# Fourth up product's operands first, bank reads first in a stage's first block, and a residual load in two halves: a fp32 decoder trunk on one core

## The chip, the core and the metric

One NeuronCore of a Trainium2 chip runs the whole program. The metric is device time in microseconds, the median of several executions; lower is better. TensorE does matrix products, VectorE (DVE) and ScalarE (ACT) do elementwise work, GpSimd (POOL) does small work and issues accumulating transfers, SyncE (SP) issues plain transfers.

## What is computed

Two decoder layers over 512 tokens of width 1024, in fp32. Layer 0 mixes with latent attention, layer 1 with banded attention; each layer ends in a squared-ReLU MLP, with a layer norm behind the mixer and one behind the MLP.

```
for l in range(2):
    y = mla(x, ...) if l == 0 else swa(x, shared_kv, ...)
    x = layernorm(alpha * x + y, ln_mix_g[l], ln_mix_b[l])
    h = relu(x @ mlp_w_up[l])            # 1024 -> 4096
    x = layernorm(alpha * x + (h * h) @ mlp_w_down[l], ln_mlp_g[l], ln_mlp_b[l])
```

## The kernel before, in words

Each fp32 operand is split into a high and a low part (`split`, L74: ACT writes the high part, DVE subtracts to give the low one), and each product is three matmuls: high by high, high by low, low by high. So a tile of weights (128x1024, 512 KB) costs a load, one ACT and one DVE instruction before TensorE can use it. The tiles pass in one `stream` through a ring of four pairs `wh`, `wl`; `weights(name)` (L295) hands out the next tile and prepares up to four ahead, but none beyond `state["hold"]`.

The order of the work on each engine is made by a scheduler ahead of the run, from priorities in program order and its own estimate of times. `tc.high_priority()` lifts instructions ahead of others that are ready; `pe(...)` and `pin(...)` keep an instruction behind what was traced before it on its engine; `behind(pair)` (L84) queues a block behind the two instructions of a split. On the chip every engine but TensorE's weight loads takes its instructions strictly in that order.

A projection back to tokens (`TokMajor`, L425) does the first 512 output columns in parts, and then in `finish` (L451) the last 512: for each block of 128 tokens 24 matmuls over four weight tiles, the addition into `xs[t]`, and the layer norm. `xs` and the norm's gain and bias `gb` come over SP. `finish` may pin the norm's DVE work (`early`).

The MLP runs in four blocks of 1024 hidden columns, each as seven products instead of eight (Strassen's scheme). An up product `U` is 48 matmuls of 256 columns, a down product `D` 24 matmuls of 512. A dash marks the block that is being begun; `FIRST_STEPS` (L40) begins with U'1 U'2 U'5 U'3 U'6 U'7 U'4 D'1 D'2, so U'3 is the fourth up product. `XFactors.turn` (L609) transposes a token block and forms the factors of U'1, U'2 and U'5; at the last one it forms those of U'3, 6, 7 and 4. Weight tiles of the sums are grown in place: POOL adds the next quarter to the raw tile by an accumulating DMA (L188) once the last split has read it. `up_out` (L694) reads the banks: for U'6 the sums L709, L710, L712, for U'7 L715, for U'4 L718. U'4 adds onto the bank of U'7, so it can't begin a half before L715 has read that half. D'1 needs the first hidden quarter (L712, then ReLU and square on ACT, L720 and L721, then the split of its factor in L730).

`begin` (L548) starts the second layer's mixer: three weight chunks by two halves of the tokens; `src.turn` puts the transposed token blocks 2 and 3 in place, which the second half reads.

Of the kernel before, what the change touches and what calls it, by code (L numbers as in the profile page):

```python
# [15 lines left out]
P = 128  # L16
# [32 lines left out]
def build(tc, nc, io, out):  # L49
    with ExitStack() as top:  # L50
# [40 lines left out]
        def pe(ins):  # L91
            tc.keep_in_program_order(ins)
# [71 lines left out]
        def queue_seven(name, key, chunk):  # L164

            quads = {}

            def half(a, jp):  # L170
                if a not in quads:
                    if (key, a) == ("U", "a"):
                        quads[a] = xp.tile([P, 4, 512], F32, tag="xt", bufs=8, name=nm("wq"))
                    elif (key, a) == ("U", "b"):
                        quads[a] = xtok.tile([P, 4, 512], F32, tag="gb", bufs=1, name=nm("wq"))
                    else:
                        quads[a] = mlp_pool[0].tile([P, 4, 512], F32, tag="quad" + a, bufs=1, name=nm("wq"))
                return quads[a][:, 2 * jp : 2 * jp + 2, :]

            def flat(ap):  # L180
                return ap.rearrange("p a b -> p (a b)")

            def grown(a, jp, *more, aside=None):
                wh, wl = tiles_of_weights(aside)
                with behind(state.pop("first", None) if (key, a, jp) == ("U", "b", 1) else None):
                    split(wh, wl, flat(half(a, jp)), keep=(a, bool(more)) == ("b", True) and key == "U")
                if more:
                    nc.gpsimd.dma_start(half(a, jp), chunk(*more, jp), accum_op=ALU.add)  # L188
                return wh, wl

            def loaded(a, jp, at, *more, aside=None):
                pe(nc.sync.dma_start(half(a, jp), chunk(*at, jp)))
                return grown(a, jp, *more, aside=aside)

            def alone(jp, aside=None):
                raw = raw_tile()
                pe(nc.sync.dma_start(raw.rearrange("p (a b) -> p a b", a=2), chunk(1, 0, jp)))
                wh, wl = tiles_of_weights(aside)
                split(wh, wl, raw)
                return wh, wl  # L200

            of = {
                1: lambda jp, aside=None: loaded("a", jp, (0, 0), 0, 1, aside=aside),
                5: lambda jp: grown("a", jp, 1, 1),
                6: lambda jp: grown("a", jp, 1, 0),
                4: lambda jp: grown("a", jp),
                2: alone,
                3: lambda jp: loaded("b", jp, (1, 1), 0, 1),
                7: lambda jp: grown("b", jp),
            }  # L210

            def add(n, asides=(None, None)):
                for jp, aside in enumerate(asides):
                    make = (lambda jp=jp, aside=aside: of[n](jp, aside)) if aside else (lambda jp=jp: of[n](jp))
                    stream.append((name, make))
                    off_ring.append(aside is not None)

            return add
# [48 lines left out]
        mlp_stream(0)  # L267
        for m in range(2):
            queue("w_k", io["w_k"][m])
        first_sq = len(stream)  # L270
        for m in range(8):
            queue("w_sq", io["w_sq"][m], nc.gpsimd if m else nc.vector)
            if m == 0:
# [151 lines left out]
        class TokMajor:  # L425
# [25 lines left out]
            def finish(self, gb=None, dst=None, early=None):  # L451

                for kp in range(4):
                    for t in range(NT):
                        if (t, kp) not in self.done:
                            self.part(t, kp)
                if gb is not None:
                    gb = gb()  # L460
                    ws = [weights(self.name) for _ in range(4)]
                    for t in range(NT):
                        n = 2 if dst is None and t == NT - 1 else 1
                        for i in range(n):
                            c = slice(i * 512 // n, (i + 1) * 512 // n)
                            b = bank(512 // n)
                            for kp in range(4):
                                self.group(b, t, kp, ws[kp], c)
                            pinned[0] = early
                            with tc.high_priority():  # L470
                                self.evac(t, slice(512 + c.start, 512 + c.stop), b)
                            pinned[0] = False
                        pinned[0] = early
                        with tc.high_priority():
                            layer_norm(t, gb, dst)
                        if early:
                            prepare(early[t])
                        pinned[0] = False
                        if dst is not None and t in (1, 2):
                            with tc.high_priority():  # L480
                                dst.turn(t - 1)
                else:
                    bs = [bank() for _ in range(NT)]
                    for kp in range(4):
                        w = weights(self.name)
                        for t in range(NT):
                            self.group(bs[t], t, kp, w)
                    for t in range(NT):
                        self.evac(t, slice(512, D), bs[t])
# [58 lines left out]
        def begin(src, chunks):  # L548


            state["hold"] = len(stream)
            ws = [weights(name) for name, _ in chunks]
            for half_ in range(2):
                cols = slice(half_ * 256, half_ * 256 + 256)
                for i, (_, evac) in enumerate(chunks):
                    b = bank(256)
                    early = half_ == 0 and i == len(chunks) - 1
                    feat_major(src, ws[i], b, cols, range(4))
                    if early:
                        with tc.high_priority():  # L560
                            src.turn(NT - 1)
                    feat_major(src, ws[i], b, cols, range(4, KD))
                    evac(cols, b)
                    if half_ == 0 and i == 1:
                        with tc.high_priority():
                            src.turn(NT - 2)


        class Factors:
# [24 lines left out]
        class XFactors(Factors):  # L594
# [14 lines left out]
            def turn(self, t):  # L609
# [18 lines left out]
                if t == NT - 1:  # L628
                    state["hold"] = len(stream)
                    quarters = [f32(self.xf[i][:, n]) for i in range(2) for n in range(2)]  # L630
                    first = split(self.part(3, 0), self.part(3, 1), self.sum(3, *quarters))
                    with behind(first):
                        for n in (6, 7, 4):
                            split(self.part(n, 0), self.part(n, 1), self.sum(n, *quarters))
                    state["first"] = first

        def mlp(src, gb, dst, mp):

# [16 lines left out]
            class Block:  # L655
# [18 lines left out]
                def up(self, n):  # L674
                    w = [weights("up") for _ in range(2)]
                    key = {3: 3}.get(n) or own_bank[n]
                    for j in range(4):

                        b = self.bank(("U", key), j // 2)
                        wh, wl = w[j // 2]  # L680
                        for k in range(4):
                            c = slice(j % 2 * 512 + k * P, j % 2 * 512 + (k + 1) * P)
                            group(
                                b[:, j % 2 * 256 : j % 2 * 256 + 256],
                                three(wh[:, c], wl[:, c], src.part(n, 0)[:, k, :], src.part(n, 1)[:, k, :]),
                                n not in (2, 4) and k == 0 and j % 2 == 0, k == 3, skip_group_check=True,
                            )
                        if j % 2:
                            self.up_out(n, j // 2)
                        if (self.q, j) == (0, 1) and n in (1, 2):  # L690
                            with tc.high_priority():
                                src.turn(n + 1)
# [80 lines left out]
            for i, (which, q, n) in enumerate(steps):  # L773
                if which == "U":
                    blocks[q].up(n)
                else:
                    blocks[q].down_(n)
                    if (q, n) == (NFF - 2, 6):
# [21 lines left out]
                    n = ((2, 1), (4, 0))[cols.start // 256][k // 4]  # L800
                    return b.fac[n][:, p, k % 4, cols.start % 256 : cols.start % 256 + P]

            if dst is not None:
                state["hold"] = first_sq
            TokMajor(Hidden(), add_last, "down").finish(gb, dst, dst and (0, 0, 0, 1))


        ed = dr.tile([SQH, BANDW], F32, name="ed")
# [290 lines left out]

        for t in range(NT):  # L1100
            xs[t] = xtok.tile([P, D], F32, tag="x", bufs=NT, name=nm("x"))
            pe(nc.sync.dma_start(xs[t], io["x"][t * P : (t + 1) * P, :]))
        gb = lambda: load_gb(io["ln_mix_g"][0], io["ln_mix_b"][0])
        x2 = Feat()
        with tc.tile_pool(name="mlp0", bufs=1) as mp:
            mlp_pool[0] = mp
# [288 lines left out]
```

## Time and profile before

| | us |
|---|---|
| median of 3 runs | 1025.76 (1025.19 to 1031.15) |
| profiled execution | 1023.86 |
| its span, first to last instruction | 1021.9 |
| TensorE busy | 994.6 (97%) |
| DVE busy | 766.6 (75%) |
| ACT busy | 555.9 (54%) |

The span is what the profile covers; 2.0 us of the profiled execution lie around it. Busy times of TensorE count overlapping matmuls once, so idle shows as a gap between the starts of two matmuls that is longer than their usual spacing.

### The profile page before, as it was taken

To read this page: it belongs to the slowest core of one execution; us is meant where nothing else is said; L and a number is where in the kernel's file an instruction comes from. 1 tells how busy PE (TensorE), PEld (TensorE's weight loads), DVE (VectorE), ACT (ScalarE), POOL (GpSimd) and SP (SyncE) were. 2 spreads that over 40 slices of the span, in tenths; PEclk is the share of its full clock that TensorE was granted. 3 is DMA by queue.
4 is the path that set the end of the run, shared out by engine and by line. 5 is a ranking of instruction groups with operands and counts; after the bars stand their busy time and mean duration, and the time that the engine had idled before them with its cause. 6 is when DMAs were issued, how large, how long until landed. Compare 5 with 4: busy or idle time off the path is not lost. (4 is left out here: it accounts for less than half of the span.)

```text
span 1021.9 us, 15865 instructions
## 1 busy us (share of the span) xinstructions
PE 994.6 (97%) x6148; PEld 895.9 (88%) x6148; DVE 766.6 (75%) x1227; ACT 555.9 (54%) x847; POOL 232.9 (23%) x204
## 2 busy tenths in 40 slices
PE   9999999989999999999999999999899999999996
PEld 8888887987999989998889898889799999998986
DVE  6588856888769858886585578688886896797756
ACT  5556643456637637646146688445654664665620
POOL 1232001312211211210014675223032122123002
PEclk9999999999999999999999999999999999999998
DMA  7421108389877976972332212349688798798332
GB/s 247 149 85 42 63 21 268 87 191 243 154 172 199 190 178 180 243 125 94 113 103 94 83 64 73 119 87 227 175 182 168 164 227 160 183 258 153 84 124 82
DMA packets 60247, 149.55 MB, mean 146 GB/s; under 512 B 5212, under 2 KB 9741, under 8 KB 60173
## 3 DMA queue, kind: packets, MB, share of 16 engines
q0 software_dynamic: 24320, 58.73, 32.1%
q1 hardware_dynamic: 35852, 89.82, 25.6%
q8 instruction: 48, 0.79, 0.3%
q14 instruction: 27, 0.21, 0.1%
HBM read 146.41 MB, written 4.22 MB: 147 GB/s over the span
## 5 line engine op out<-in xcount | busy, mean ns | idle before, releaser
L103 PE MATMUL mm<-wh,fac 128*128 128x512 f32 (+1 forms) x944 | 295.5, 390 | 4.6 <-ACT fac L76 3.0
L76 ACT ACTIVATE wh<-wq 128x1024 fp32r<-128x1024 f32 x164 | 173.5, 1060 | 202.5 <-PE mm L103 136.2
L79 DVE TENSOR_TENSOR wl<-wq,wh 128x1024 fp32r<-128x1024 f32 x164 | 199.7, 1221 | 80.4 <-ACT wh L76 79.3
L103 PE MATMUL mm<-xth,wh 128*128 128x256 f32 (+1 forms) x936 | 245.1, 290 | 5.3 <-DVE a L715 5.3
L103 PE MATMUL mm<-xth,wl 128*128 128x256 f32 (+1 forms) x808 | 234.7, 290 | 1.2 <-DVE wl L79 1.2
L103 PEld LDWEIGHTS mm<-wh,fac 128*128 128x128 f32 x944 | 177.6, 190 | 41.6 <-ACT fac L76 3.4
L103 PE MATMUL mm<-xtl,wh 128*128 128x256 f32 (+1 forms) x680 | 198.7, 292 | 0.0
L103 PE MATMUL mm<-wl,fac 128*128 128x512 f32 (+1 forms) x472 | 183.3, 388 | 0.0
L103 PEld LDWEIGHTS mm<-xth,wh 128*128 128x128 f32 x936 | 170.1, 192 | 8.5 <-issue 5.6
L103 PEld LDWEIGHTS mm<-xth,wl 128*128 128x128 f32 x808 | 154.7, 192 | 3.7 <-DVE wl L79 1.4
L188 POOL DMA_DIRECT2D wq<-in_up x64 | 77.5, 1218 | 277.1 <-DVE wl L79 209.7
L76 ACT ACTIVATE wh<-raw 128x1024 fp32r<-128x1024 f32 (+4 forms) x85 | 84.7, 998 | 98.1 <-PE mm L103 66.8
L103 PEld LDWEIGHTS mm<-xtl,wh 128*128 128x128 f32 x680 | 130.2, 191 | 3.0
L79 DVE TENSOR_TENSOR wl<-raw,wh 128x1024 fp32r<-128x1024 f32 (+3 forms) x64 | 75.6, 1189 | 38.9 <-ACT wh L76 38.8
L103 PEld LDWEIGHTS mm<-wl,fac 128*128 128x128 f32 x472 | 89.6, 190 | 17.1
L188 POOL DMA_DIRECT2D wq<-in_down x48 | 42.0, 875 | 188.1 <-DVE wl L79 168.9
L375 POOL TENSOR_TENSOR rs<-v,half 128x1 f32<-128x1 f32 x24 | 28.8, 1200 | 192.8 <-DVE v L394 156.5
L79 POOL TENSOR_TENSOR wl<-raw,wh 128x1024 fp32r<-128x1024 f32 (+2 forms) x21 | 43.8, 2090 | 79.5 <-ACT wh L76 77.0
L103 PE MATMUL mm<-wh,oh 128*128 128x512 f32 x128 | 50.9, 398 | 1.3 <-ACT wh L76 1.3
L103 PE MATMUL mm<-wl,oh 128*128 128x512 f32 x128 | 50.0, 390 | 0.8 <-DVE wl L79 0.8
L103 PE MATMUL mm<-wh,ol 128*128 128x512 f32 x128 | 50.0, 391 | 0.0
L532 DVE TENSOR_TENSOR x<-mm,x 128x512 f32<-128x512 f32 (+1 forms) x49 | 32.9, 675 | 13.9 <-PE mm L103 13.6
(218 smaller groups left out, 1845.1 us busy)
## 6 DMA issues: line engine op xcount, KB each, us to landing
wq<-in_up POOLq DMA_DIRECT2D x64, 512.0 KB, 7.6
wq<-in_down POOLq DMA_DIRECT2D x48, 512.0 KB, 6.5
wq<-in_up SPq DMA_DIRECT2D x32, 512.0 KB, 5.6
raw<-in_down SPq DMA_DIRECT2D x28, 512.0 KB, 6.8
wq<-in_down SPq DMA_DIRECT2D x24, 512.0 KB, 6.2
raw<-in_up SPq DMA_DIRECT2D x16, 512.0 KB, 4.0
raw<-in_w_o SPq DMA_DIRECT2D x8, 512.0 KB, 3.2
raw<-in_w_sq SPq DMA_DIRECT2D x8, 512.0 KB, 3.3
```

Source lines behind the costliest of these rows:

```text
L76: high = nc.scalar.activation(dst_h, src, AF.Copy)
L79: low = (engine or nc.vector).tensor_sub(dst_l, src, f32(dst_h))
L103: pe(nc.tensor.matmul(dst, st, mv, start=first and i == 0, stop=last and i == len(pairs) - 1, **kw))
L188: nc.gpsimd.dma_start(half(a, jp), chunk(*more, jp), accum_op=ALU.add)
L375: nc.gpsimd.tensor_tensor(r, v, half, ALU.pow)
L532: nc.vector.tensor_add(xs[t][:, c], b, xs[t][:, c])
```

## The change

Five edits. (1) U'3's second weight tile is now queued behind the split of U'3's factor, and the factors of U'6, U'7 and U'4 are formed in a new `rest()`, called after U'5 and queued behind that tile's split. Before, all of them stood behind U'3's factor. (2) In the first block (`self.q == 0`) `up_out` is traced at high priority. (3) The residual `x` of layer 0 is loaded as eight half rows: the first 512 columns as before, the later ones from `gb()`, which `finish` now calls after the first of its four `weights`. (4) The finish of the MLP of layer 0 no longer passes `early`, so its norm isn't pinned, and no longer sets the stream's `hold` to the first `w_sq` tile; `begin` no longer sets `hold`. (5) `begin` transposes token block 3 after the third chunk, where before it stood in that chunk's middle.

```diff
             def grown(a, jp, *more, aside=None):
                 wh, wl = tiles_of_weights(aside)
-                with behind(state.pop("first", None) if (key, a, jp) == ("U", "b", 1) else None):
-                    split(wh, wl, flat(half(a, jp)), keep=(a, bool(more)) == ("b", True) and key == "U")
+                first = state.pop("first", None) if (key, a, jp) == ("U", "b", 1) else None
+                with behind(first):
+                    pair = split(wh, wl, flat(half(a, jp)), keep=(a, bool(more)) == ("b", True) and key == "U")
+                if first:
+                    state["second"] = pair
...
-        first_sq = len(stream)
...
                 if gb is not None:
+                    ws = [weights(self.name)]
                     gb = gb()
-                    ws = [weights(self.name) for _ in range(4)]
+                    ws += [weights(self.name) for _ in range(3)]
...
         def begin(src, chunks):
-            state["hold"] = len(stream)
             ws = [weights(name) for name, _ in chunks]
             for half_ in range(2):
                 cols = slice(half_ * 256, half_ * 256 + 256)
                 for i, (_, evac) in enumerate(chunks):
                     b = bank(256)
-                    early = half_ == 0 and i == len(chunks) - 1
-                    feat_major(src, ws[i], b, cols, range(4))
-                    if early:
+                    feat_major(src, ws[i], b, cols)
+                    evac(cols, b)
+                    if half_ == 0 and i > 0:
                         with tc.high_priority():
-                            src.turn(NT - 1)
-                    feat_major(src, ws[i], b, cols, range(4, KD))
-                    evac(cols, b)
-                    if half_ == 0 and i == 1:
-                        with tc.high_priority():
-                            src.turn(NT - 2)
+                            src.turn(i + 1)
...
-                    first = split(self.part(3, 0), self.part(3, 1), self.sum(3, *quarters))
-                    with behind(first):
-                        for n in (6, 7, 4):
-                            split(self.part(n, 0), self.part(n, 1), self.sum(n, *quarters))
-                    state["first"] = first
+                    state["first"] = split(self.part(3, 0), self.part(3, 1), self.sum(3, *quarters))
+
+            def rest(self):
+
+                quarters = [f32(self.xf[i][:, n]) for i in range(2) for n in range(2)]
+                with behind(state.pop("second")):
+                    for n in (6, 7, 4):
+                        split(self.part(n, 0), self.part(n, 1), self.sum(n, *quarters))
...
                         if j % 2:
-                            self.up_out(n, j // 2)
+                            with tc.high_priority() if self.q == 0 else ExitStack():
+                                self.up_out(n, j // 2)
...
                     blocks[q].up(n)
+                    if (q, n) == (0, 5):
+                        src.rest()
...
-            if dst is not None:
-                state["hold"] = first_sq
-            TokMajor(Hidden(), add_last, "down").finish(gb, dst, dst and (0, 0, 0, 1))
+            TokMajor(Hidden(), add_last, "down").finish(gb, dst)
...
-            pe(nc.sync.dma_start(xs[t], io["x"][t * P : (t + 1) * P, :]))
-        gb = lambda: load_gb(io["ln_mix_g"][0], io["ln_mix_b"][0])
+            pe(nc.sync.dma_start(xs[t][:, 0:512], io["x"][t * P : (t + 1) * P, 0:512]))
+
+        def gb():
+            for t in range(NT):
+                pe(nc.sync.dma_start(xs[t][:, 512:D], io["x"][t * P : (t + 1) * P, 512:D]))
+            return load_gb(io["ln_mix_g"][0], io["ln_mix_b"][0])
```

## Rows read from the trace of the kernel before

**Rows 1.** The page, busy us and share of the span by engine

```profile
PE 994.6 (97%) x6148; PEld 895.9 (88%) x6148; DVE 766.6 (75%) x1227; ACT 555.9 (54%) x847; POOL 232.9 (23%) x204
```

**Rows 2.** Waits of TensorE, whole span: us in total, times, longest us

```profile
PE mm L103 <- DVE a L715: 5.3, 2, 2.7
PE mm L103 <- ACT fac L76: 3.0, 2, 1.5
```

**Rows 3.** Timeline of TensorE, last tile of `w_o`: start us, us, instruction, [idle before]

```profile
168.14 0.39 PE L103 MATMUL mm<-wh,ol 128*128 128x512 f32 x1
...
171.42 0.39 PE L103 MATMUL mm<-wh,ol 128*128 128x512 f32 x1
...
172.78 0.39 PE L103 MATMUL mm<-wh,ol 128*128 128x512 f32 x1
```

**Rows 4.** Timeline of SP's queue in the same stage

```profile
153.54 2.54 SPq L1102 DMA_DIRECT2D x<-in_x  x4
157.36 0.33 SPq L140 DMA_DIRECT2D raw<-in_w_o  x1
...
159.07 0.44 SPq L140 DMA_DIRECT2D raw<-in_w_o  x1
```

**Rows 5.** Timeline of ACT in the same stage

```profile
168.72 1.06 ACT L76 ACTIVATE wh<-raw 128x1024 fp32r<-128x1024 f32 x1 [3.65 <-DMA raw<-in_w_o]
```

**Rows 6.** Windows: busy by engine, then clock, DMA share, GB/s

```profile
157.00:161.00 4.00, 4.00 (x19) 3.30 (x18) 2.15 (x3) 0.39 (x1) 0.00 (x0) 1.00 0.97 356
...
219.00:223.00 4.00, 4.00 (x36) 4.00 (x35) 2.71 (x3) 1.17 (x2) 0.03 (x1) 1.00 1.13 208
...
238.50:242.00 3.50, 3.29 (x8) 2.62 (x9) 2.43 (x3) 2.51 (x3) 0.00 (x0) 0.51 0.49 151
...
733.00:737.00 4.00, 3.70 (x9) 2.96 (x10) 3.75 (x4) 2.68 (x4) 0.00 (x0) 0.57 0.49 145
```

**Rows 7.** Timeline of TensorE, layer 0, U'7 to the next block

```profile
221.15 0.28 PE L103 MATMUL mm<-xth,wh 128*128 128x256 f32 x1
...
226.79 0.28 PE L103 MATMUL mm<-xth,wl 128*128 128x256 f32 x1
229.68 0.48 PE L103 MATMUL mm<-xth,wh 128*128 128x256 f32 x2 [2.62 <-DVE a L715]
...
237.16 0.50 PE L103 MATMUL mm<-wh,fac 128*128 128x512 f32 x1 [1.50 <-ACT fac L76]
...
250.79 0.28 PE L103 MATMUL mm<-xth,wh 128*128 128x256 f32 x1
```

**Rows 8.** Timeline of DVE in the same stretch

```profile
226.52 1.22 DVE L79 TENSOR_TENSOR wl<-wq,wh 128x1024 fp32r<-128x1024 f32 x1
...
228.86 0.68 DVE L715 TENSOR_TENSOR a<-uv,mm 128x512 f32<-128x512 f32 x1
...
230.59 0.68 DVE L712 TENSOR_TENSOR a<-mm,uv 128x512 f32<-128x512 f32 x1
```

**Rows 9.** Timeline of ACT in the same stretch

```profile
231.31 2.01 ACT L720 ACTIVATE a<-a 128x1024 f32<-128x1024 f32 x2 [2.93 <-DVE a L712]
...
236.06 1.99 ACT L76 ACTIVATE fac<-a 128x1024 fp32r<-128x1024 f32 x2
```

**Rows 10.** Timeline of TensorE, layer 1, U'7 to the next block

```profile
721.31 0.28 PE L103 MATMUL mm<-xth,wl 128*128 128x256 f32 x1
...
745.47 0.28 PE L103 MATMUL mm<-xth,wh 128*128 128x256 f32 x1
```

**Rows 11.** Timeline of TensorE in `begin`

```profile
529.10 0.39 PE L103 MATMUL mm<-xth,wl 128*128 128x256 f32 x1 [1.20 <-DVE wl L79]
...
531.74 1.25 PE L411 MATMUL tr<-ident,x 128*128 128x128 f32 x8 [1.19 <-DVE xtl L79]
```

**Rows 12.** Timeline of DVE in `begin`, last norm and splits

```profile
526.63 1.28 DVE L400 SCALAR_TENSOR_TENSOR x<-x,rs,gb 128x1024 f32<-128x1024 f32 x1
527.83 2.35 DVE L79 TENSOR_TENSOR wl<-raw,wh 128x1024 fp32r<-128x1024 f32 x2
```

## The prediction

> **What bounds the kernel now.** I read the page first: TensorE is busy 97% of the span, the next engine 75% [rows 1]. So the kernel is TensorE's matmuls plus the places where they stand still, and a change that adds or removes no matmul, as this one, can move little more than those places hold. The waits of TensorE name them [rows 2]: two waits of 2.7 us at most on L715, two on the factor written by ACT. That list undercounts, because it leaves out the time after a wait in which TensorE runs at half clock. So I went to the timeline and took the distance between starts instead.
>
> A matmul of 256 columns starts 0.120 us after the last (221.15 to 226.79 holds 47) [rows 7], one of 512 columns 0.227 us (171.42 to 172.78 holds 6) [rows 3]. With these two spacings three places stand out that the diff touches.
>
> First, the last tile of `w_o`: from 168.14 to 171.42 lie three spacings, 0.68 us, but it took 3.28: 2.6 us lost [rows 3]. Its ACT split waited 3.65 us for the transfer [rows 5], which SP issued at 159.07 and which landed 9.6 us later; ahead of it in the queue stand 2 MB of `x`, a tile of `w_o` and 1 MB of `gb` [rows 4]. The memory system moved 356 GB/s there, so the queue and not the issue is what is late [rows 6].
>
> Second, the end of the first MLP block in layer 0. From U'7's last start, 226.79, to the next block's first, 250.79, are 24.0 us. The work in it is one spacing, 48 matmuls of U'4 and 48 of D'1 and D'2: 0.12 + 5.76 + 10.90 = 16.8. So 7.2 us are lost [rows 7]. 2.8 of them lie ahead of U'4, which waits for L715 [rows 7]. L715 stands in DVE's order behind the split of U'4's second tile, the first L712 and an L710; the split alone runs 226.52 to 227.66, L715 only at 228.86 [rows 8]. U'7's first half was in the bank by about 224.0 (221.15 and 24 spacings). The other 4.4 us lie in D'1 and D'2: the second L712 comes at 230.59 [rows 8], ACT's chain ends in the factor at 236.06 [rows 9], D'1 starts at 237.16 [rows 7], and behind these two gaps the granted clock is 0.51, the lower level of 1.2 GHz, from 238.5 to 242 [rows 6]. A matmul there takes twice its time, so about 1.7 us of the 4.4 are clock.
>
> Third, the same place in layer 1: 721.31 to 745.47 is 24.16, less 16.8 is 7.4 us lost [rows 10], with the clock at 0.57 from 733 to 737 [rows 6].
>
> Together 17.2 us. Only these can be won by edits 1 to 3; edits 4 and 5 touch a fourth place, `begin`, with two waits of 1.2 us [rows 11].
>
> **The change part by part.** *The residual in halves.* Ahead of the last `w_o` tile there now stand 1 MB of `x` and one tile, and no `gb`. Issued at 159.07 or a little before (it waits for its raw buffer as before), it shares the queue with one other tile issued at 157.36 [rows 4]; 1.05 MB at 356 GB/s are 2.9 us, so it lands by about 162, and with ACT's 1.06 us [rows 5] and a DVE split of 1.2 [rows 8] it is ready by 165, ahead of 168.1. Gain 2.6 us, between 0 and 2.6. What hides the late half of `x` and `gb`: from 157.36 two tiles of `w_o`, one of U'1, 1 MB of `x` and 1 MB of `gb` are 3.7 MB, 10.3 us, so all is in by about 167.7, while the first token block's norm can start only when its 24 matmuls end, about 169.6 without the stall (172.2 less 2.6). Cover of 2 us; past it each microsecond costs one. The SP queue gets four more issues of 0.64 us [rows 4], 2.5 us, which lie beside transfers that take longer.
>
> *Bank reads first.* No instruction is added. L715 should go as soon as DVE is free behind U'7's first half. But the order is written ahead by the scheduler, and in the order before, the split of U'4's second tile comes ahead of reads that were ready earlier, so the scheduler takes that tile as early. On the chip it isn't: the DMA engines are full from 219 to 223 (share 1.13) [rows 6]. If the split keeps its place ahead of L715, the read starts at 227.66, ends at 228.34, and U'4 starts at 228.5 with the lag of before (228.86 + 0.68 to 229.68, 0.14): a wait of 1.6 in place of 2.8, 1.2 won. If L710 and L712 stay between too, nothing is won; if the split falls behind, all 2.8. I take 1.2, the nearest to the order of before. L712 moves further: the second one no longer stands behind the split of D'1's first tile, and can go about 2 us earlier, which moves ACT's ReLU, square and factor with it. D'1 then starts when U'4 ends, and without its gaps the clock should stay up. Of 4.4 I take 4.0 (0.4 left for the low part of the factor); the low bound is that the chain moves its 2.3 us and the clock still falls, the high bound 4.4. So 5.2 per layer, 2.3 to 7.2; 10.4 for both.
>
> *U'3's tile ahead of the other factors.* TensorE doesn't stand at U'3 or U'6 now, so nothing is won there directly. Two DVE and two ACT instructions change places; the factors of U'6 come one split of 1.2 us later in order, and U'7's second accumulating transfer is issued earlier into a full queue. Zero, hidden under U'3's 5.8 us (48 spacings); if the cover failed, U'6 would wait one split, 1.2 us per layer (bounds -2.4 to 0).
>
> *`begin` and the lost pins.* Token block 3 is transposed 12 matmuls, 1.4 us, later in order. Now those 12 matmuls wait 1.2 us for a split that runs 527.83 to 530.2 behind the pinned norm, and the transposes another 1.2 [rows 11, 12]. Without pins that split may go earlier and both waits shrink; or the second half waits for the transposed block, about 1.3 of ACT and DVE on 512 columns. Loss to gain -2 to +2; I take 0.
>
> Sum: 2.6 + 10.4 + 0 = 13.0 us off the profiled execution's 1023.86 (span 1021.9 and 2.0 around it), giving 1010.9; the median of the three runs lies 1.9 above that execution, so 1012.8 in its terms.
>
> A rule of the Trainium skill speaks against edit 3. The rows: four pieces of `x` of 512 KB were issued in 2.54 us [rows 4], and the stage ran at 356 GB/s with several in flight [rows 6], so I charge bytes only. The Trainium skill, "DMA: Bandwidth & Descriptors", section on the anatomy of one DMA, gives each transfer about 2.0 us of fixed cost plus its bytes at 436 GB/s. By that, in sequence, eight pieces would take about 21 us where four take 13, an estimate from that page, and `gb` would come 8 us later. The rows show overlapping transfers instead.
>
> **The rivals.**
> *A, the forecast*: 1012.8; its own range 1008 to 1017.
> *B, the splits stay ahead of the reads.* For it: the full DMA engines and the order before. The wait ahead of U'4 stays, D'1's chain moves by 2.3 per layer: 2.6 + 4.6 = 7.2, so 1018.6.
> *C, `begin` or the smaller pieces take part back.* The norm of layer 0's MLP orders badly, or `gb` lands past its 2 us of cover: 2 to 3 us of the 13 return, 1015 to 1016. Against it: both have cover today.
> *D, other side: reads first starve the weights.* DVE takes its order strictly; a read placed ahead of a split waits for TensorE, and the split behind it, ACT 1.06 and DVE 1.2, is then exposed. Four tiles late in a layer (two of U'4, two of D'1) are 9.2 us against the 7.4 won at most: plus 1.9 per layer, less 2.6, gives 1027; it decides when more than three tiles in a layer come late, and with every tile of U'6 to D'2 it would pass 1036. Against it: DVE has a quarter of its time free [rows 1].
> *E, the order doesn't change.* The scheduler had the reads as early as it could: only 2.6 won, 1023.
>
> **How the numbers follow.** A 0.58, B 0.18, C 0.10, D 0.09, E 0.05. Range: best case 2.6 + 14.4 + 2 off is 1006.8, and up to E's edge with the low bounds 1021: 1007 to 1021 leaves out D and E and a little of A, under 2 in 10. One per cent is 10.3 us, about what a measurement of this kernel can tell from no change: faster than 1015.5 is most of A (0.54) and half of C: 0.59. Slower than 1036 is D's tail and what I can't see in a reordered schedule: 0.07. The rest, 0.34, lies within.
>
> **What would show it.** Right: no wait on ACT before the last `w_o` tile and no gap over 0.5 us in that group; L715 directly behind a split or ahead of it, U'4 starting within 1.7 us of U'7's end; no wait on ACT's factor ahead of D'1 and a clock of 1.00 there in both layers; `begin` within 2 us of before. Wrong: L715's wait still over 2.5 us (B, E), TensorE waiting for `wl` in U'4 or D'1 (D), the first norm waiting for `gb` (C), or new gaps in a place that the diff doesn't touch.

## The result, and the profile after

| | median, us | runs | ratio to before | 95% interval |
|---|---|---|---|---|
| before | 1026.18 | 19 | | |
| after | 1030.71 | 19 | 1.0046 | 1.0032 to 1.0059 |

The change made the kernel 0.46% slower, about 4.5 us; the forecast was 1012.8 us, 13.0 faster, and the time lies outside its range. The profiled execution of after took 1028.9 us with a span of 1027.1; that of before has a span of 1021.9, so the two traces lie 5.2 us apart.

The waits of TensorE over the whole span of after, to be read beside [rows 2] (in total, times, longest):

```profile
PE mm L103 <- DVE a L716: 5.1, 2, 2.8
PE mm L103 <- ACT fac L76: 4.9, 2, 2.4
PE mm L103 <- DVE wl L79: 4.3, 4, 2.1
```

L716 is L715 of before: the wait that edit 2 was to shorten is as long as it was. The factor's wait went up from 3.0 to 4.9.

**The last tile of `w_o`.** TensorE, then ACT and DVE in after (start us, us, instruction, idle before):

```profile
169.34 0.39 PE L103 MATMUL mm<-wh,ol 128*128 128x512 f32 x1
169.94 0.50 PE L103 MATMUL mm<-wh,oh 128*128 128x512 f32 x1 [0.22 <-ACT wh L76]
172.58 0.50 PE L103 MATMUL mm<-wl,oh 128*128 128x512 f32 x1 [2.13 <-DVE wl L79]
172.92 0.39 PE L103 MATMUL mm<-wh,ol 128*128 128x512 f32 x1
...
167.88 1.06 ACT L76 ACTIVATE w_fac<-wq 128x1024 fp32r<-128x1024 f32 x1 [3.83 <-DMA wq<-in_up]
168.85 1.04 ACT L76 ACTIVATE wh<-raw 128x1024 fp32r<-128x1024 f32 x1
...
168.98 1.23 DVE L79 TENSOR_TENSOR w_fac<-wq,w_fac 128x1024 fp32r<-128x1024 f32 x1 [1.87 <-ACT w_fac L76]
...
171.31 1.22 DVE L79 TENSOR_TENSOR wl<-raw,wh 128x1024 fp32r<-128x1024 f32 x1
```

From 169.34 to 172.92 are 3.58 us, three spacings are 0.68, so 2.9 us are lost where 2.6 were [rows 3]. But the reason is another. In before ACT waited for `w_o`'s own transfer [rows 5]. In after it waits 3.83 us for `w_fac<-wq`, the first tile of U'1, which TensorE doesn't need before 192 us, and the last tile of `w_o` is split behind it, with no wait of its own. On DVE `w_fac` stands ahead of it too. The same turn of the order stands in layer 1, ahead of the last tile of `w_so`, where before lost nothing:

```profile
666.38 1.06 ACT L76 ACTIVATE w_fac<-wq 128x1024 fp32r<-128x1024 f32 x1 [3.33 <-DMA wq<-in_up]
667.34 1.04 ACT L76 ACTIVATE wh<-raw 128x1024 fp32r<-128x1024 f32 x1
...
671.13 0.50 PE L103 MATMUL mm<-wl,oh 128*128 128x512 f32 x1 [1.05 <-DVE wl L79]
```

**The end of the first block, layer 0.** TensorE, DVE and ACT of after, and the clock in a window (columns as in [rows 6]):

```profile
228.33 0.28 PE L103 MATMUL mm<-xth,wl 128*128 128x256 f32 x1
231.41 0.47 PE L103 MATMUL mm<-xth,wh 128*128 128x256 f32 x2 [2.80 <-DVE a L716]
...
239.83 0.80 PE L103 MATMUL mm<-wh,fac 128*128 128x512 f32 x1 [2.44 <-ACT fac L76]
...
254.37 0.28 PE L103 MATMUL mm<-xth,wh 128*128 128x256 f32 x1
...
228.25 1.23 DVE L79 TENSOR_TENSOR wl<-wq,wh 128x1024 fp32r<-128x1024 f32 x1
229.39 0.68 DVE L713 TENSOR_TENSOR a<-mm,uv 128x512 f32<-128x512 f32 x1
229.99 0.68 DVE L711 TENSOR_TENSOR uv<-mm,uv 128x512 f32<-128x512 f32 x1
230.59 0.68 DVE L716 TENSOR_TENSOR a<-uv,mm 128x512 f32<-128x512 f32 x1
...
237.79 1.04 ACT L76 ACTIVATE wh<-raw 128x1024 fp32r<-128x1024 f32 x1
238.74 1.99 ACT L76 ACTIVATE fac<-a 128x1024 fp32r<-128x1024 f32 x2
...
242.00:246.00 4.00, 4.00 (x11) 3.13 (x10) 2.44 (x3) 1.82 (x2) 0.00 (x0) 0.50 0.81 245
```

DVE's order is that of [rows 8], line for line: the split of U'4's second tile (228.25), then L713 (L712 of before), L711, and only then the read L716. On ACT one split of a raw tile more (237.79) stands ahead of the factor than in before [rows 9], and D'1's wait is 2.44 us where it was 1.50 [rows 7]. From U'7's last start, 228.33, to the next block's first, 254.37, are 26.0 us; less 16.8 of work, 9.2 are lost, 2.0 more than before [rows 7], and the granted clock is 0.50, the level of 1.2 GHz, from 242 to 246. In layer 1 it is 7.3, as before [rows 10].

How much of the 2.0 us comes from the changed order one trace can't say. The kernel with edit 2 alone (below) has before's instruction order on every engine, and between the same two matmuls its trace has

```profile
227.85 0.28 PE L103 MATMUL mm<-xth,wl 128*128 128x256 f32 x1
...
253.36 0.28 PE L103 MATMUL mm<-xth,wh 128*128 128x256 f32 x1
```

25.5 us, so 8.7 are lost there too, against before's 7.2.

So 0.3 us more are lost at `w_o`, 2.0 in the first block, 1.3 at `w_so`. `begin` took 0.7 less. About 1.3 us lie in the softmax tail from 622 to 645 us, and 1.2 us ahead of the `w_o` stage (168.14 against 169.34 for the same matmul), where TensorE, ACT and DVE run the same instructions in the same order in both.

### The profile page after: what moved, and what is told of

It reads as the page before. It is cut to its first block, busy times and chain, and to the rows that moved or that the text cites. A ratio compares the mean times of both kernels' runs of the same rounds, so it can differ in the third digit from the quotient of the medians.

```text
span 1027.1 us, 15873 instructions
## 1 busy us (share of the span) xinstructions
PE 996.0 (97%) x6148; PEld 895.4 (87%) x6148; DVE 766.3 (75%) x1227; ACT 554.5 (54%) x847; POOL 232.6 (23%) x204
## 5 line engine op out<-in xcount | busy, mean ns | idle before, releaser
L535 DVE TENSOR_TENSOR x<-mm,x 128x512 f32<-128x512 f32 (+1 forms) x49 | 32.9, 674 | 14.1 <-PE mm L103 13.8
```

The lines of the kernel that those rows point to most:

```text
L535: nc.vector.tensor_add(xs[t][:, c], b, xs[t][:, c])
```

## The experiments

Theory at the start: after lost its time where the scheduler, given other inputs, put ACT's and DVE's instructions in another order, and the bank reads never moved. Rivals: the smaller transfers cost what is missing; the factors or the turns in `begin` do.

### Each edit alone

**The high priority of the bank reads** (edit 2):

```
-    self.up_out(n, j // 2)
+    with tc.high_priority() if self.q == 0 else ExitStack():
+        self.up_out(n, j // 2)
```

> The bank reads' high priority alone, on the kernel before. Order theory (the changed kernel lost its time where instructions of ScalarE and VectorE stand in another order): this edit moves no instruction of any engine, so 0 us, within 1 us of before, and U'4's wait stays near 2.8 us in layer 0. The prediction's step (b): 10.4 us faster. Rival 'reads first starve the weights': slower by 5 us or more.

Measured 1025.17 us, ratio 0.9994 (0.9979 to 1.0010). The built program has the same instructions in the same order as before on all five engines; and the changed kernel without this edit has the order of the changed kernel. U'4 waits as ever for the same read (L716 here):

```profile
PE mm L103 <- DVE a L716: 4.8, 2, 2.5
```

What follows: edit 2 does nothing, and with it went 10.4 of the forecast's 13.0 us.

**U'3's second tile ahead** (edit 1; the other factors put behind it):

```
-    first = split(self.part(3, 0), ...)
-    with behind(first): (the factors of U'6, U'7, U'4)
+    state["first"] = split(self.part(3, 0), ...)
+    def rest(self):      # called after U'5
+        with behind(state.pop("second")): (the same factors)
```

> U'3's second tile ahead of the other factors, alone. Order theory: ScalarE now has the squares and both raw tiles' splits ahead of the factor that D'1 waits for, so D'1's wait grows from 1.5 to about 2.4 us in each layer, and a little more goes at the lower clock behind it: 2 to 3 us slower. The prediction's step (c): 0 us.

Measured 1026.93 us, ratio 1.0010 (0.9992 to 1.0028). ACT's order is that of after at D'1, and the factor's wait grew to 1.97 and 1.98 us from 1.50 and 1.49. The time agrees with nothing as well as with 2 us; the expectation's size was too large, its sign isn't shown by the time. At the two ends of the first blocks 9.4 and 9.0 us are lost in this trace; in traces with before's order of ACT and DVE there, 7.2 to 8.8 in layer 0 and 6.6 to 8.4 in layer 1.

**One weight tile ahead of the norm's loads** (part of edit 3):

```
+    ws = [weights(self.name)]
     gb = gb()
-    ws = [weights(self.name) for _ in range(4)]
+    ws += [weights(self.name) for _ in range(3)]
```

> Only the first of a finish's weight tiles queued ahead of the norm's two loads. Order theory: in layer 0 the last w_o tile keeps its place ahead of U'1's first tile on ScalarE and is loaded earlier, so its stall of 2.6 us falls to 0.8 to 1.5; in layer 1's w_so stage U'1's first tile moves ahead of the last w_so tile and costs about 1.3 us; together 0 us, -1 to +1. Rival 'transfers': nothing changes in layer 1, 1 to 2 us faster.

Measured 1025.51 us, ratio 0.9998 (0.9982 to 1.0014). Its last `w_o` tile on ACT and TensorE:

```profile
166.76 1.06 ACT L76 ACTIVATE wh<-raw 128x1024 fp32r<-128x1024 f32 x1 [0.21 <-DMA raw<-in_w_o]
168.05 1.06 ACT L76 ACTIVATE w_fac<-wq 128x1024 fp32r<-128x1024 f32 x1 [0.23 <-DMA wq<-in_up]
...
170.19 0.50 PE L103 MATMUL mm<-wl,oh 128*128 128x512 f32 x1 [0.58 <-DVE wl L79]
```

Here `w_o` keeps its place, is split 2 us earlier than in [rows 5], and the stall is 0.9 us instead of 2.6. In layer 1 the order is turned and 1.0 us is lost at `w_so`. Both as expected, and the sum is nothing.

**The same with x in halves** (the whole of edit 3):

```
-    pe(nc.sync.dma_start(xs[t], io["x"][rows of t, :]))
+    pe(nc.sync.dma_start(xs[t][:, 0:512], io["x"][rows of t, 0:512]))
     ...
+    (in gb(), ahead of the norm's loads) the four loads of columns 512 to 1023
```

> As the run before it, and x loaded in two halves of 512 columns, the later behind w_o. Order theory: now U'1's first tile stands ahead of the last w_o tile on ScalarE in layer 0 too, so its stall stays at 2.6 to 2.9 us, and layer 1 loses 1.3 us as well: 1.3 to 2 us slower than before, and slower than the run with the weight tile alone. The prediction's step (a): 2.6 us faster. Rival 'smaller pieces': the four loads more delay the weight tiles behind them, 1 us or so slower with the stall at another tile than the last of w_o.

Measured 1030.16 us, ratio 1.0040 (1.0023 to 1.0057): nearly all of what after lost. ACT, TensorE and the clock:

```profile
162.59 1.06 ACT L76 ACTIVATE wh<-raw 128x1024 fp32r<-128x1024 f32 x1 [4.14 <-DMA raw<-in_w_o]
168.32 1.06 ACT L76 ACTIVATE w_fac<-wq 128x1024 fp32r<-128x1024 f32 x1 [4.67 <-DMA wq<-in_up]
169.29 1.04 ACT L76 ACTIVATE wh<-raw 128x1024 fp32r<-128x1024 f32 x1
...
173.02 0.50 PE L103 MATMUL mm<-wl,oh 128*128 128x512 f32 x1 [2.14 <-DVE wl L79]
...
175.00:177.00 2.00, 2.00 (x6) 1.63 (x5) 1.90 (x5) 1.76 (x2) 0.56 (x1) 0.50 1.10 249
```

The halves do bring `w_o` early: the tile before the last is split at 162.59. But the order is now turned in layer 0 too, the stall is 3.5 us by the spacings, and behind it the granted clock falls to 0.50 and 1.6 us more are lost. 5.1 us against before's 2.6, and 1.3 at `w_so`: 3.8 us at these two places, and 4.0 by the medians. The trace's whole span is 7.5 us longer than before's; of the rest 1.5 lie in `begin` and 1.0 in the first 15 us. The direction was expected, the size was twice as large. The clock's part, which wasn't counted, is 1.6 us in this trace, but it isn't this edit's alone: in the kernel with only the reads first, below, a stall of 3.2 us at `w_o` in before's order was followed by a granted clock of 0.50, too.

**The turns in `begin`** (edits 4 and 5, the old order of the transposes and no holds):

```
-    state["hold"] = len(stream)          # and the hold of first_sq, early=
-    feat_major(src, ws[i], b, cols, range(4)); src.turn(NT - 1) ...
+    feat_major(src, ws[i], b, cols); evac(cols, b); src.turn(i + 1)
```

> The turns in `begin` back after whole pieces and the holds removed, alone. Order theory: begin's lost time falls from 2.9 to about 2.0 us and the softmax tail at 620 to 645 us changes with the order of its instructions, by 0 to 2 us either way: -1 to +1 us. The prediction's step (d): 0 us, -2 to +2. Rival 'the pins matter': more than 2 us slower.

Measured 1027.06 us, ratio 1.0005 (0.9992 to 1.0019). `begin` takes 0.7 us less than in before, the softmax tail 0.5 more. Nothing in sum, as step (d) had it.

**The changed kernel without edit 3:**

> The changed kernel without the edits to x and to the order of the finish's weight tile. Order theory: what the changed kernel lost came with these two, so it is within 1.5 us of before (1025 to 1028 us), U'4's and D'1's stalls as in the changed kernel. Rival 'the loss is in the factors or the turns': it stays near 1030 us.

Measured 1027.70 us, ratio to its own runs of before (1025.07) 1.0030 (1.0014 to 1.0047). The median lies in the expected band, but the interval excludes no loss, so edit 3 isn't all of it: edits 1, 4 and 5 cost 1.4 to 4.8 us together. Edit 3 alone cost 4.0 by the medians, this kernel 2.6, and after only 4.5: the parts don't add up, and how they overlap isn't shown. The factor's wait is the row that stands out:

```profile
PE mm L103 <- ACT fac L76: 4.4, 2, 2.4
```

### The edits made to do what they say

**The weight order held, with x in halves.** On top of edit 3, U'1's first tile is issued behind the last tile of `w_o` or `w_so`:

```
-    split(wh[:, c], wl[:, c], raw[:, c], low)
+    state["last"] = split(wh[:, c], wl[:, c], raw[:, c], low)
     ...
+    with behind(state.pop("last", None) if aside else None):
         split(wh, wl, flat(half(a, jp)), ...)
```

> The x halves and the weight tile ahead of the norm's loads, with the split of U'1's first tile told to stand behind that of the last w_o (and w_so) tile. Order theory: the w_o stall of 2.6 us goes down to 0 to 0.8, nothing is lost at w_so, 2 to 3 us faster than before and 6 us faster than the halves without that order. Rival 'smaller pieces': the last w_o tile is late whatever the order, the stall stays above 2 us and the time within 1 us of before.

Measured 1028.46 us, ratio 1.0018 (1.0004 to 1.0032): slower, against the expectation. ACT, DVE and TensorE:

```profile
165.82 1.06 ACT L76 ACTIVATE wh<-raw 128x1024 fp32r<-128x1024 f32 x1 [1.37 <-PE mm L103]
...
175.11 1.06 ACT L76 ACTIVATE w_quada<-wq 128x1024 fp32r<-128x1024 f32 x1 [5.39 <-DMA wq<-in_up]
...
179.66 1.07 ACT L76 ACTIVATE xth<-tr 128x512 fp32r<-128x512 f32 x2
...
180.28 0.69 DVE L79 TENSOR_TENSOR xtl<-tr,xth 128x512 fp32r<-128x512 f32 x1 [2.05 <-ACT xth L76]
...
184.77 1.07 PE L621 MATMUL tr<-ident,x 128*128 128x128 f32 x8 [1.67 <-DVE x L401]
```

The half of the expectation on the stall came true: the last tile is split at 165.82, waiting only for TensorE to give its buffer free, and no matmul of `w_o` waits. But U'1's second tile, issued behind the four late loads, comes late and holds ACT for 5.39 us; the split of the first transposed tokens stands behind it, DVE's next norm behind that, and TensorE waits 1.67 us for that norm. 1.9 us of the 2.6 are given back in this trace, and the softmax tail loses 0.5 more than in before. The trace's span is 3.9 us longer than before's, and the rows put most of it away from the edited place: 1.1 us in the first 15 us, and 1.8 and 0.9 at the ends of the two first blocks, where 9.0 and 8.3 us are lost. That is near the 8.8 and 8.4 that before's order reaches in other traces. In the two later kernels with x in halves and this order held, ACT waits as long for that tile, 5.45 and 5.50 us, and only 0.2 us are given back. Why this kernel isn't faster than before stays open.

**The reads really first,** and nothing else, on the kernel before. In the first block, VectorE's half of U'4's second tile is not emitted with its tile, but behind the first read of U'7's bank:

```
+    if first_block and (a, jp, more) == ("a", 1, ()):      # U'4's second tile
+        nc.scalar.activation(wh, src, AF.Copy)
+        state["late"] = lambda: nc.vector.tensor_sub(wl, src, f32(wh))
     ...
-    nc.vector.tensor_sub(self.quarter(done)[:, pairs], self.v[:, pairs], of(7))
+    read = nc.vector.tensor_sub(self.quarter(done)[:, pairs], self.v[:, pairs], of(7))
+    if "late" in state:
+        with tc.issue_after(read.ins), tc.high_priority():
+            state.pop("late")()
```

> The bank reads really first: in the first block VectorE's half of the split of U'4's second tile is issued behind the read of U'7's first bank, and nothing else is changed. The prediction's step (b), with the edit doing what it says: U'4's wait 2.8 to 1.6 us or less in each layer, D'1's stall and the low clock behind it mostly gone, 2 x 5.2 us faster (2.3 to 7.2 each). Order theory: the same sign, but U'4's second tile and D'1's tiles are now split later, so some comes back as waits on wl: 1 to 4 us per layer. Rival 'reads first starve the weights': no gain, PE waits on wl instead.

Measured 1014.94 us, ratio 0.9900 (0.9877 to 0.9923): 11.5 us by the medians, 10.3 by the ratio. DVE, TensorE and the clock:

```profile
230.49 0.68 DVE L714 TENSOR_TENSOR uv<-tr,uv 128x512 f32<-128x512 f32 x1
...
232.28 0.67 DVE L720 TENSOR_TENSOR a<-uv,mm 128x512 f32<-128x512 f32 x1
232.88 0.68 DVE L717 TENSOR_TENSOR a<-mm,uv 128x512 f32<-128x512 f32 x1
...
234.61 1.22 DVE L188 TENSOR_TENSOR wl<-wq,wh 128x1024 fp32r<-128x1024 f32 x1
...
233.10 0.47 PE L103 MATMUL mm<-xth,wh 128*128 128x256 f32 x2 [0.65 <-DVE a L720]
236.57 0.48 PE L103 MATMUL mm<-xth,wh 128*128 128x256 f32 x2 [0.36 <-ACT a L729]
...
242.00:246.00 4.00, 4.00 (x19) 3.30 (x19) 3.99 (x5) 3.21 (x4) 0.00 (x0) 1.00 1.07 285
```

Six reads stand in a row (229.89 to 233.56 us), the splits follow (L188 is the held one), U'4 waits 0.65 us and its second half 0.36, D'1 doesn't wait, and the granted clock stays at 1.00. At the ends of the first blocks 1.5 and 1.2 us are lost, where before lost 7.2 and 7.4. No wait on `wl` takes their place here, so the rival of starved weights falls. (The profiled execution took 1019.85 us, 5 more than the median; the `w_o` stage, whose order this kernel leaves as it was, lost 4.8 us in it, and `begin` took 2.7 more than in before.)

**Both together:**

> Both of the two kernels before this in one: halves of x with the weight order held, and the reads really first. Order theory: the sum of both, 4 to 11 us faster than before. Rival: one stall is only moved behind the other, and the sum is less than the larger of the two.

Measured 1013.05 us, ratio 0.9877 (0.9854 to 0.9900), more than the 4 to 11 us expected. The halves with their order held add about 2 us to the reads, with intervals that overlap.

**The changed kernel with the reads really first** (in place of the high priority):

> The changed kernel with one edit made to do what it says: in place of the high priority, VectorE's half of U'4's second tile is issued behind the read of U'7's first bank. Order theory (step (b) was priced rightly and only never happened): 10 to 12 us faster than the changed kernel, 1018 to 1021 us, the stalls at w_o and w_so still there. Rival 'the other edits use up the gain': above 1024 us.

Measured 1016.63 us, ratio to before 0.9919 (0.9896 to 0.9943): 14 us below the changed kernel's median, which is of other runs, and more than the 10 to 12 expected. D'1's longer wait of after is gone with the rest. The `w_o` stall is still there, 2.3 us, and 1.2 at `w_so`.

**The same with the weight order held:**

> As the run before it, and U'1's first tile told to stand behind the last w_o and w_so tile. Order theory: what the prediction added up, 1012 to 1016 us. Rival: 1018 us or more, the halves of x make the norm's loads late instead and nothing of their 2.6 us is kept.

Measured 1012.87 us, ratio 0.9885 (0.9859 to 0.9910). TensorE in both layers:

```profile
224.79 0.28 PE L103 MATMUL mm<-xth,wl 128*128 128x256 f32 x1
226.62 0.36 PE L103 MATMUL mm<-xth,wh 128*128 128x256 f32 x1 [1.55 <-DVE a L721]
...
243.93 0.28 PE L103 MATMUL mm<-xth,wh 128*128 128x256 f32 x1
...
716.66 0.28 PE L103 MATMUL mm<-xth,wl 128*128 128x256 f32 x1
717.99 0.36 PE L103 MATMUL mm<-xth,wh 128*128 128x256 f32 x1 [1.05 <-DVE a L721]
...
735.30 0.28 PE L103 MATMUL mm<-xth,wh 128*128 128x256 f32 x1
```

Less 16.8 us of work, 2.3 us are lost in layer 0 and 1.8 in layer 1, where before lost 7.2 and 7.4 [rows 7, 10]: 10.5 won. No matmul of `w_o` or `w_so` waits.

**Without the halves of x.** The kernel before with the reads first, the weight tile ahead of the norm's loads and the weight order held:

> The kernel before with the reads really first, the weight tile ahead of the norm's loads and the weight order held, but x loaded whole: the halves are left out. Order theory: the norm's loads are in time again, a w_o stall of about 0.9 us stays, 1012 to 1014 us, within 1 us of the kernel with the halves. If the halves carry a gain of their own it is 2 us slower than that.

Measured 1010.44 us, ratio 0.9867 (0.9842 to 0.9893): the fastest, 1.3% below before and, by the medians of separate runs, 2.0% below after. Its ACT:

```profile
163.81 1.06 ACT L76 ACTIVATE wh<-raw 128x1024 fp32r<-128x1024 f32 x1 [6.01 <-DMA raw<-in_w_o]
165.09 1.06 ACT L76 ACTIVATE wh<-raw 128x1024 fp32r<-128x1024 f32 x1 [0.21 <-DMA raw<-in_w_o]
...
170.30 1.06 ACT L76 ACTIVATE w_quada<-wq 128x1024 fp32r<-128x1024 f32 x1 [2.82 <-DMA wq<-in_up]
```

With x loaded whole no matmul of `w_o` waits in this trace either, and ACT splits U'1's second tile 3 to 7 us earlier than in the three kernels with halves and the order held. The time lies below the expected 1012 to 1014, and the expected stall of 0.9 us isn't there; ACT and DVE have the order of the run with the weight tile alone at this place, where 0.9 were lost, so that difference is one between executions. With halves and all else the same it was 1013.05, with intervals that overlap: the halves show no gain of their own. Putting one weight tile ahead of 1 MB of the norm's loads, with the order held, did as well.

## Why the prediction was wrong, point by point

**What bounds the kernel: right.** In the trace of the fastest kernel the three places lose 14.3 us less than in before, and its span is 14.1 shorter: the gain came from the 17.2 us of standing still that the prediction had counted.

**Step (b), bank reads first: the step that failed, and not in its price.** The prediction said that L715 "should go as soon as DVE is free" and weighed how far the scheduler would move it; its sum rests on a high priority moving it at all. It moved nothing: the 10.4 us of this step didn't come. The price was about right: 5.2 us per layer were forecast, and 4.9 and 5.6 were won in the changed kernel, 5.7 and 6.2 in the kernel before, once a dependency put the reads first. The way there was another. The 1.2 us at U'4 were forecast with the split still ahead of the read; the dependency put it behind, for which the prediction allowed all 2.8. U'4's wait then lay between 0.65 and 1.55 us in layer 0, and that 1.55 is close to the forecast 1.6 is luck: there the read stands behind four other bank reads, and no longer behind that split. Rival E, "the order doesn't change", is what happened to the reads, and was given 0.05; its 1023 us left out what edit 3 would cost. Why the scheduler ignores the priority was not tried. That its own timeline has the split's data ready before the bank is the prediction's own inference from [rows 6, 8]; if a priority chooses only among what is ready, which no run here shows, that inference already spoke against a gain.

**Step (a), x in halves: right on the transfers, wrong on the order in which the tiles are split.** The tiles of `w_o` did arrive early. The step costed bytes and never asked in which order ACT and DVE would split them; U'1's first tile went ahead of the last of `w_o`, and the stall changed its cause and kept its size. A strict order could be read in [rows 8], where DVE stands behind one split. The Trainium skill, "PSUM — Partial Sum Buffer", section on engine and sequencer instructions, says that the queues of ScalarE and VectorE are strictly first in, first out; the trace agrees, with 3.83 us of ACT's wait for a tile that nobody needs yet and `wh` behind it without a wait of its own. The turn in `finish` also holds for `w_so`, which the part-by-part working didn't cost: 1.3 us.

**The cover of 2 us for the late loads: too thin in one trace of three.** With the order held, the first norm wasn't late, but U'1's second tile behind the four loads was, and in one trace gave 1.9 us back by way of ACT's order, in two others with the same order 0.2. That is rival C, by a path that it hadn't named.

**The page weighed against it.** The Trainium skill, "DMA: Bandwidth & Descriptors", section on the anatomy of one DMA, gives its fixed cost and its rate for transfers issued by GpSimd. The pieces of `x` are issued by SP, and the prediction's estimate of 8 us later for the norm's loads carries those figures over. The trace doesn't show such a delay: with the halves and the order held the first norm started without a wait on a transfer. What it shows is later issue: SP issued U'1's second tile at 165.75 us, against 161.67 with x whole.

**Step (c), U'3's tile: zero in sum was about right, for a reason not seen.** The edit left U'3 and U'6 as they were, but changed ACT's order at D'1, far behind, where one raw tile more stands ahead of the factor: 0.5 us more wait per layer alone, 0.9 in after. The time of that edit alone doesn't tell it from nothing.

**Step (d), `begin`: right.** 0.7 us less there, nothing in the median.

**The sum.** With the two orders held, the changed kernel takes 1012.87 us, where 1012.8 was forecast. That it agrees so closely is partly luck: in its trace the three places give 2.6 and 10.5 us, but `begin` and the softmax tail take 1.2 and 1.0 more than in before, and the profiled executions lie 10.6 apart. Still it says where the miss lies: what the scheduler does with each edit, not what the edit is worth. The changed kernel as it stands missed the 10.4 of step (b) and the 2.6 of step (a), and lost 4.5 besides; edit 3 alone cost 4.0 and the changed kernel without it 2.6, so how that loss divides stays open. A slip in rival D changes nothing: four tiles of 1.06 and 1.2 us are 9.0, not 9.2, so its 1027 is 0.6 too high.

## What to carry to other kernels

Where a scheduler writes the order, an edit that asks it for a preference has to be read back from the built instruction order before any price is put on it; where the order matters, say it with a dependency on the one instruction that has to go first. When a transfer is made earlier, look at which instructions wait for transfers on the splitting engine, and in which order: an engine in strict order gives the gain to the first of them, needed or not. And an edit to one helper changes each stage that calls it. Before a stage's loss in one trace is put down to an edit, look at the same stage in a trace of another kernel that has the same order there: here the end of layer 1's first block lost 6.6 to 8.4 us in six traces with the same order of ACT and DVE.

## What had not been expected

Two executions whose instructions stand in the same order differ from the first microseconds on: U'1's first matmul of layer 0 started at 190.45 us in the trace of before and here, with the priorities alone, at

```profile
191.51 0.28 PE L103 MATMUL mm<-xth,w_fac 128*128 128x256 f32 x1
```

1.06 us later, all of it lost by 13 us. Single traces therefore compare stage by stage, not by their spans. And a stall of 2.9 us at `w_o` left the granted clock of the matmuls behind it at 1.00 in after, where one of 3.5 us at the same place in the kernel with edit 3 alone was followed by 0.50 for 2 us:

```profile
175.00:177.00 2.00, 2.00 (x10) 1.68 (x9) 1.93 (x4) 1.38 (x2) 1.01 (x1) 1.00 1.09 247
```

(This is after's window.) There 0.6 us more of standing still came with 1.6 us more lost at the lower clock. But the length of the waits alone doesn't tell the two cases apart. In `begin`, waits of 1.29 and 1.20 us were followed by a granted clock of 0.59 (530 to 534 us) in the kernel with only the reads first, waits of 1.19 and 1.36 us by 1.00 in the fastest kernel. The one took 2.7 us more than before in that place, the other 0.2. So what the lower clock costs in one trace is no price of an edit.
